# The residual behind layer 0's MLP, added by GpSimd's DMA for two of three token chunks

## The chip, the cores and the metric

The kernel runs on one core of a Trainium2 chip. A core has a matrix engine (TensorE, PE in the profile), a vector engine (VectorE, DVE), a scalar engine (ScalarE, ACT), GpSimd (POOL) and SyncE (SP), each with an instruction queue of its own that is worked off in order, and 16 DMA engines that SP, ACT and POOL can start. The metric is the device time of one execution in microseconds (us).

## What is computed

A two-layer decoder trunk over 1040 tokens (16 learned ones and 1024 of x) and 1024 channels. Each layer is a token mixer and a squared-ReLU MLP, both between RMS norms, and each with a residual. Layer 0 mixes with RWKV-7 and pooling, layer 1 with differential attention. What matters here is the last line of the loop in layer 0 and the first of layer 1:

```python
for i in range(DEPTH):
    hn = rmsnorm(h, g[0])
    m = rwkv_pool_mixer(hn, ...) if i % 2 == 0 else diff_attn_mixer(hn, ...)
    h = h + rmsnorm(m, g[1])
    f = sq_relu_mlp(rmsnorm(h, g[2]), mlp_w1[i], mlp_w2[i])
    h = h + rmsnorm(f, g[3])          # the residual of this document, for i = 0
```

## The kernel before

Tokens lie along the free dimension and channels along the partitions, so that h is eight blocks of 128 channels by 1040 tokens. All matmuls are done in three products of halves (high times high, low times high, high times low), and each operand is therefore cut into a high and a low half.

`late` does the part of a layer from its output projection to the end of its MLP. It does not issue instructions directly: each step is a task of `Flow`, with an engine, a cost, and lists of the pieces that it reads and writes. `Flow.order` then writes down an order for all engines at once: it always takes the task that can start earliest, and of those that can start at the same time the one with the longest way to the end (its rank; a task can be given extra length with `tail`). A DMA counts there with 0.42 us of its queue, then its bytes at 350 GB/s, and 2.0 us more until its data can be used. The order is fixed when the kernel is built; on the chip each engine waits in that order for whatever it needs.

Layer 0's MLP ends in `ac0` and `ac1` (`acc` in the code), 4 blocks of channels each. The end of `late` works in three chunks of tokens (`CH`: 348, 346 and 346, here chunk 0, 1 and 2), and for each of them:

- `down(q)` adds the last product to `ac` (L1053) and sums the squares of the result over the channels (L682 on ACT, L683 on DVE).
- `finish(q)` loads the residual h of the chunk from DRAM into the tiles `hh` with two DMAs of SP (L1062), forms the norm's factor (`rsqrt`, L741 to L743 on ACT, L747 and L748 on DVE), and for each of the eight blocks k multiplies by gain and factor (L1072, DVE) and adds the residual (L1073, DVE). After every second block the two finished blocks are stored to DRAM (L1077), from ACT for chunks 1 and 2.
- `squares(q)` starts the sum of squares for layer 1's first norm: for chunk 0 through the matrix engine, for chunks 1 and 2 block by block into the tile `rsa` (L677 or L682 on ACT, then L683 on DVE).
- `normed(c)` makes layer 1's input: the high halves (L1107, ACT) and the low halves (L1108, DVE). These tasks have a `tail` of 40, 30 and 20 us for chunks 0, 1 and 2, so all that leads to them goes ahead of `squares`, and chunk 1 ahead of chunk 2.

The calls stand in the order `down(0)`, then for each chunk c: `down(c + 1)`, `finish(c)`, `squares(c)`, `normed(c)`. The norm factors of chunk 1 use two small tiles that the squares of `down(2)` use as well, so `finish(1)` begins behind the last square of `down(2)`.

`mixer1` follows, outside `Flow`. Its instructions are ordered by the scheduler of the language; those of `late` keep their order among themselves. Its first matmuls (L377 to L379) project q, k and v of head 0 chunk by chunk. `settle` (L485, with L459 to L463) closes the sum of squares of chunk 1, later of chunk 2, with a matmul over `rsa`. The low half of q's weights (tile `wpx`) is made by the only POOL instruction near this place, L362, which reads two tensors in SBUF.

Of the kernel before, what the change touches and what calls it, by code (L numbers as in the profile page):

```python
# [10 lines left out]
ALU = mybir.AluOpType  # L11
# [3 lines left out]
P = 128  # L15
# [306 lines left out]
class Trunk:  # L322
# [231 lines left out]
    def late(self, l, xs, part, hin, hmid, hout, pre, rsb):  # L554

        nc, tc, A = self.nc, self.tc, self.A
        tt, stt = nc.vector.tensor_tensor, nc.vector.scalar_tensor_tensor
# [13 lines left out]
        def later(make, dt, n):  # L571
            made = {}

            def get(i):
                if i not in made:
                    made[i] = make(i, dt)
                return made[i]

            return [Later(lambda i=i: get(i)) for i in range(n)]

        def use(x):
            return x() if isinstance(x, Later) else x
# [9 lines left out]
        H = [big(i, F32) for i in (0, 1)]  # L592
# [29 lines left out]
        def nC(e, mt, u, v):  # L622
            return [("A", e, mt, a) for a, b in cells if a < v and b > u]

        def nA(e, k):
            return nC(e, k // 2, k % 2 * NH, k % 2 * NH + NH)
# [5 lines left out]
        def nH(i):  # L632
            return [("H", i, k) for k in range(4)]
# [24 lines left out]
        m = AC  # L658
        F = Flow(tc)
# [38 lines left out]
        def free_up(b):  # L698
            held.difference_update(x[1:] for x in b[1])
# [36 lines left out]
        def rsqrt(acc, names, n, y0, t0, ny, nt):  # L736
            vw = sv if len(acc.shape) == 3 else (lambda t: t)

            def a():
                y, t = vw(use(y0)), vw(use(t0))  # L740
                nc.scalar.activation(y, acc, AF.Ln, scale=1.0 / 1024, bias=self.con[:, K_EPS:K_EPS + 1])  # L741
                nc.scalar.activation(y, y, AF.Exp, scale=-0.5)
                nc.scalar.activation(t, y, AF.Square)  # L743

            def v():
                y, t = vw(use(y0)), vw(use(t0))
                stt(t, acc, 1e-6 * 1024, t, op0=ALU.add, op1=ALU.mult)  # L747
                stt(y, t, -3.0 * 1024, y, op0=ALU.add, op1=ALU.mult)  # L748

            F.act(3 * n, a, r=names, w=[ny, nt], k=3)  # L750
            F.dve(2 * n, v, r=names + [ny, nt], w=[ny, nt], k=2)
# [80 lines left out]
        def raw_load(src):  # L832
            r = self.nraw % 2
            self.nraw += 1
            t = R[r]
            F.dma(lambda: nc.sync.dma_start(t.rearrange("p m n -> p (m n)"), src), P * 8192, w=[("R", r, 0), ("R", r, 1)])
            return t, r
# [63 lines left out]
        def weight(i, raw, r, n):  # L901

            a = {(i, e): raw[:, i, 512 * e:512 * e + n] for i in (0, 1) for e in (0, 1)}
            s0, s1 = S[0][:, :n], S[1][:, :n]
            r0, r1 = [("R", r, 0)], [("R", r, 1)]
            if i == 1:
                F.dve(n, lambda: tt(s0, a[1, 0], a[1, 1], op=ALU.add), r=r1, w=[("S", 0)])
                F.dve(n, lambda: tt(s1, s0, a[0, 0], op=ALU.subtract), r=r0 + [("S", 0)], w=[("S", 1)])
                F.dve(n, lambda: tt(a[1, 0], a[0, 0], a[1, 0], op=ALU.subtract), r=r0 + r1, w=r1)
            if i == 3:  # L910
                F.dve(n, lambda: tt(s1, a[0, 1], s1, op=ALU.subtract), r=r0 + [("S", 1)], w=[("S", 1)])
            src, rd = {1: (a[0, 0], r0), 6: (s1, [("S", 1)]), 5: (s0, [("S", 0)]), 2: (a[0, 1], r0),
                       7: (a[1, 0], r1), 3: (s1, [("S", 1)]), 4: (a[1, 1], r1)}[i]
            return one(slot(), src, n, rd)
# [3 lines left out]
        for j in range(14):  # L918
# [4 lines left out]
            raw, r = raw_load(w1[j])  # L923
# [16 lines left out]
            for i in (1, 2, 5, 6, 3, 7, 4) if j == 0 else order:  # L940
                w = weight(i, raw, r, 512)
# [15 lines left out]
            both, nb = flat(ev[:, 1:3]), nA(e, 1) + nA(e, 2)  # L957
# [8 lines left out]
        acc = AC  # L966
# [3 lines left out]
        H3 = later(big, F32, 2)  # L970
# [5 lines left out]
        for b in range(4):  # L976
            nk = 4 if b < 3 else 2
            for q, i in enumerate(order):
                p = place[was[q]]
# [11 lines left out]
            for mp in range(4):  # L991
                raw, r = raw_load(w2[b, mp])
# [10 lines left out]
                for i in order:  # L1003
                    w = weight(i, raw, r, P * nk)
# [6 lines left out]
        for mp in range(4):  # L1011
            r = self.nraw % 2
# [45 lines left out]
        def finish(q):  # L1058
            t0, W = ends[q]
            u, v = t0 - off, t0 - off + W  # L1060
            for x in (0, 1):
                F.dma(lambda x=x: nc.sync.dma_start(use(H3[x][:, :, :W]), self.rows(hmid, t0, W)[:, 4 * x:4 * x + 4]), P * 16 * W, w=nH(x))  # L1062
            a, names = self.sums[q]
            y, t, ny, nt = TT[2][:, :W], T3[1][:, :W], ("T", 2), ("T", 1)
            if q == len(ends) - 1:
                y, t, ny, nt = S[1 - q % 2][:, :W], S[q % 2][:, :W], ("S", 1 - q % 2), ("S", q % 2)
            rsqrt(a, names, W, y, t, ny, nt)
            free_up(self.sums[q])
            rows = self.rows(hout, t0 - off, W)
            for k in range(KT):  # L1070
                d, nd = chunk(k, u, v), nC(k // 4, k % 4, u, v)
                F.dve(W, lambda d=d, k=k: stt(d, d, self.gcol(l, 3, k), y, op0=ALU.mult, op1=ALU.mult), r=nd + [ny], w=nd)  # L1072
                F.dve(W, lambda d=d, k=k: tt(d, d, use(H3[k // 4][:, k % 4, :W]), op=ALU.add), r=nd + [("H", k // 4, k % 4)], w=nd)  # L1073
                if k % 2:
                    src = acc[k // 4].rearrange("p (m h) t -> p m (h t)", h=2)[:, (k - 1) % 4:k % 4 + 1, u:v]
                    other = k % 4 == 3 if l else q > 0
                    F.dma(lambda src=src, k=k, other=other: (nc.scalar if other else nc.sync).dma_start(rows[:, k - 1:k + 1], src), P * 8 * W,  # L1077
                          r=nC((k - 1) // 4, (k - 1) % 4, u, v) + nd, w=[("out", q, k)], eng="ACT" if other else "SP")

        if l:  # L1080
            for q in range(4):
                down(q)
                finish(q)
            F.run()
            stack.close()
            pre.close()
            return None
# [31 lines left out]
        for c in range(3):  # L1119
            if c < 2:  # L1120
                down(c + 1)
            finish(c)
            squares(c)
            normed(c)
# [960 lines left out]
```

## Time and profile before

| What | us |
|---|---|
| median of 3 runs | 2776.96 |
| lowest and highest of them | 2776.26, 2778.88 |
| the profiled execution | 2771.01 |
| its span, from the first to the last instruction | 2769.1 |

All rows below come from the profiled execution and count from the start of its span. A row of the timeline gives start, duration, engine, line of the kernel, operation, the tile written, the tile read, the shape and, in brackets, how long the engine had been idle and who released it. Neighbouring instructions of one kind are merged into one row with a count. "SPq" and "ACTq" are the queues' own DMA instructions.

### The profile page before, as it was taken

What the parts mean: (1) busy time and instruction counts of PE and PEld (TensorE: products, weight loads), DVE (VectorE), ACT (ScalarE), POOL (GpSimd) and SP (SyncE); (2) the same over time, 40 slices, a digit from 0 to 9 for tenths busy, and PEclk for the clock granted to TensorE, in tenths of its full rate; (3) what the DMA queues carried; (4) which work ended last, traced back from release to release, by engine and by line L of the source; (5) the groups of instructions that cost most, each with busy time, mean ns of one, the idle gap of its engine ahead of it and who ended that gap; (6) DMA issues with size and microseconds to landing.
All of it is one profiled execution on the core that took longest, in us unless ns stands there. A gap on an engine that the chain in (4) does not pass through costs nothing.

```text
span 2769.1 us, 44824 instructions
## 1 busy us (share of the span) xinstructions
PE 2614.2 (94%) x16950; PEld 2381.9 (86%) x16950; DVE 2032.5 (73%) x3742; ACT 1342.7 (48%) x2779; POOL 290.4 (10%) x410
## 2 busy tenths in 40 slices
PE   7999998899999999999968999999889999999997
PEld 6899897899899999999956899898787788778877
DVE  5356876534977777888786887888648778778888
ACT  5456776544633334343344556555636333443342
POOL 0111334220000000000012222222000000000000
PEclk9999998899999999999988999999999999999998
DMA  4456777554324345443332222222243243543443
GB/s 152 172 183 187 244 220 222 179 162 150 142 101 170 137 164 193 169 153 132 107 112 73 59 77 68 62 67 62 77 159 137 103 167 150 194 172 137 152 160 122
DMA packets 198575, 391.27 MB, mean 141 GB/s; under 512 B 59984, under 2 KB 122328, under 8 KB 185944
## 3 DMA queue, kind: packets, MB, share of 16 engines
q1 hardware_dynamic: 171176, 348.24, 37.8%
q10 hardware_dynamic: 27184, 40.18, 4.0%
q8 instruction: 133, 2.18, 0.3%
q14 instruction: 82, 0.67, 0.1%
HBM read 240.06 MB, written 131.38 MB: 134 GB/s over the span
## 4 chain that ended last, share of the span: by engine, by line
PE 64%; DVE 10%; ACT 4%; issue 2%; DMA 2%; POOL 0%; DVEq 0%; SPq 0%; ACTq 0%; POOLq 0%
PE bank L691 44%; PE psq L377 2%; PE psq L378 2%; PE psq L379 2%; PE ps L292 1%; PE s L1824 1%; PE tr L1870 1%; PE s L1826 1%; PE xs L292 1%; ACT p L1843 1%; DVE ac L1072 1%; DVE ac L1073 1%; DVE opb L818 1%; PE av L1896 1%; DVE ac L1001 1%
## 5 line engine op out<-in xcount | busy, mean ns | idle before, releaser
L691 PE MATMUL bank<-opa,wp 128*128 128x260 f32 (+1 forms) x3296 | 658.9, 320 | 8.6 <-DVE wp L782 5.3
L691 PEld LDWEIGHTS bank<-opa,wp 128*128 128x128 f32 x3296 | 518.0, 189 | 60.1 <-DVE wp L782 6.8
L691 PE MATMUL bank<-opb,wp 128*128 128x260 f32 (+1 forms) x1150 | 348.4, 324 | 1.8 <-DVE ac L1001 1.8
L292 PE MATMUL ps<-opa,whi 128*128 128x346 f32 (+2 forms) x1008 | 268.3, 328 | 4.7 <-DVE ys L292 4.0
L691 PE MATMUL bank<-opa,hh 128*128 128x260 f32 (+1 forms) x1112 | 241.1, 321 | 8.0 <-DVE hh L782 5.3
L691 PEld LDWEIGHTS bank<-opb,wp 128*128 128x128 f32 x1150 | 216.9, 189 | 21.0 <-ACT opa L1024 2.2
L1001 DVE TENSOR_TENSOR ac<-bank,ac 128x520 f32<-128x520 f32 (+1 forms) x256 | 171.6, 691 | 67.8 <-PE bank L691 66.5
L691 PE MATMUL bank<-opa,opb 128*128 128x260 f32 (+4 forms) x1168 | 206.1, 306 | 11.6 <-ACT opb L670 7.2
L691 PEld LDWEIGHTS bank<-opa,hh 128*128 128x128 f32 x1112 | 185.9, 191 | 24.4 <-DVE hh L782 5.8
L691 PEld LDWEIGHTS bank<-opa,opb 128*128 128x128 f32 x1168 | 168.2, 194 | 22.6 <-ACT opb L670 7.6
L292 PEld LDWEIGHTS ps<-opa,whi 128*128 128x128 f32 x1008 | 181.1, 192 | 6.5 <-DVE ys L292 4.8
L691 PE MATMUL bank<-opb,hh 128*128 128x260 f32 (+1 forms) x616 | 180.6, 327 | 0.0
L781 ACT CAST wp<-raw 128x512 fp32r<-128x512 f32 (+1 forms) x138 | 80.3, 584 | 184.6 <-PE bank L691 179.0
L292 PE MATMUL ps<-opa,wlo 128*128 128x346 f32 (+2 forms) x504 | 158.4, 314 | 0.0
L781 ACT CAST wp<-ss 128x512 fp32r<-128x512 f32 (+1 forms) x130 | 76.7, 590 | 164.5 <-PE bank L691 143.6
L1843 ACT ACTIVATE p<-s,m 128x272 f32<-128x272 f32 (+7 forms) x128 | 95.4, 750 | 85.4 <-DVE m L1839 83.6
L691 PE MATMUL bank<-opa,tt 128*128 128x260 f32 (+1 forms) x648 | 130.5, 318 | 0.2 <-DVE tt L782 0.2
L691 PEld LDWEIGHTS bank<-opb,hh 128*128 128x128 f32 x616 | 117.7, 191 | 9.9
L377 PE MATMUL psq<-opa,wp 128*128 128x346 f32 (+2 forms) x352 | 117.5, 334 | 4.4 <-DVE rp L462 2.6
L362 POOL TENSOR_TENSOR wpx<-raw,wp 128x1024 fp32r<-128x1024 f32 (+1 forms) x14 | 34.4, 2459 | 785.8 <-PE bank L691 742.8
L379 PE MATMUL psq<-opa,wp 128*128 128x346 f32 (+2 forms) x352 | 113.4, 322 | 0.0
L691 PE MATMUL bank<-opb,opb 128*128 128x256 f32 (+4 forms) x456 | 111.3, 308 | 0.5 <-DVE tt L747 0.5
(408 smaller groups left out, 6561.9 us busy)
## 6 DMA issues: line engine op xcount, KB each, us to landing
raw<-in_w_dram SPq DMA_DIRECT2D x64, 1024.0 KB
hid<-ac SPq DMA_DIRECT2D x14, 1820.0 KB
hid<-ac SPq DMA_DIRECT2D x14, 1792.0 KB
hh<-hid SPq DMA_DIRECT2D x23, 1040.0 KB
hh<-hid SPq DMA_DIRECT2D x23, 1024.0 KB
pk<-sg ACTq DMA_DIRECT2D x32, 704.0 KB
lt<-pk SPq DMA_DIRECT2D x32, 704.0 KB
raw<-in_w_qkv_dram SPq DMA_DIRECT2D x24, 512.0 KB
```

What stands on the lines that cost most here:

```text
L292: one = eng, cost, lambda: fn(*args, **kw), r, w
L362: (lo or nc.gpsimd).tensor_tensor(lw[:, :n], raw[:, :n], hi[:, :n].bitcast(F32), op=ALU.subtract)
L377: nc.tensor.matmul(ps, wh, xh, start=(first and i == 0), stop=False)
L378: nc.tensor.matmul(ps, wl, xh, start=False, stop=False)
L379: nc.tensor.matmul(ps, wh, xl, start=False, stop=(last and i == n - 1))
L691: nc.tensor.matmul(ps, use(x), use(y), start=start and i == j == 0, stop=i == len(ws) - 1 and j == 2, skip_group_check=not start)
L781: F.act(n, lambda: nc.scalar.copy(use(t[0][:, :n]), src), r=rd, w=[z[0]] + claim)
L818: F.dve(4 * NH, lambda: tt(lo, use(src), hi.bitcast(F32), op=ALU.subtract), r=rd + wh, w=wl)
L1001: F.dve(NH, lambda d=d, q=q: tt(sv(d), q, sv(d), op=ALU.add), r=nq + nd, w=nd, ps=True)
L1072: F.dve(W, lambda d=d, k=k: stt(d, d, self.gcol(l, 3, k), y, op0=ALU.mult, op1=ALU.mult), r=nd + [ny], w=nd)
L1073: F.dve(W, lambda d=d, k=k: tt(d, d, use(H3[k // 4][:, k % 4, :W]), op=ALU.add), r=nd + [("H", k // 4, k % 4)], w=nd)
L1843: nc.scalar.activation(p[:, :L0], S[c][:, :L0], AF.Exp, bias=m2[:, c:c + 1], scale=0.125, accum_out=m2[:, 2 + c:3 + c])
```

## The change

For chunks 1 and 2 of layer 0, `finish` no longer loads h into `hh` and no longer adds it on DVE. After every second block a DMA started by GpSimd reads two blocks of h from DRAM and adds them to the two blocks in `ac`, in place. The store of the two blocks, `squares` and `normed` then wait for that DMA. Chunk 0, and layer 1, are as before.

```diff
         def finish(q):
             t0, W = ends[q]
             u, v = t0 - off, t0 - off + W
+            plus = not l and q in (1, 2)
             for x in (0, 1):
-                F.dma(lambda x=x: nc.sync.dma_start(use(H3[x][:, :, :W]), self.rows(hmid, t0, W)[:, 4 * x:4 * x + 4]), P * 16 * W, w=nH(x))
+                if not plus:
+                    F.dma(lambda x=x: nc.sync.dma_start(use(H3[x][:, :, :W]), self.rows(hmid, t0, W)[:, 4 * x:4 * x + 4]), P * 16 * W, w=nH(x))
...
                 F.dve(W, lambda d=d, k=k: stt(d, d, self.gcol(l, 3, k), y, op0=ALU.mult, op1=ALU.mult), r=nd + [ny], w=nd)
-                F.dve(W, lambda d=d, k=k: tt(d, d, use(H3[k // 4][:, k % 4, :W]), op=ALU.add), r=nd + [("H", k // 4, k % 4)], w=nd)
+                if plus:
+                    if k % 2:
+                        both = acc[k // 4].rearrange("p (m h) t -> p m (h t)", h=2)[:, (k - 1) % 4:k % 4 + 1, u:v]
+                        nb = nC((k - 1) // 4, (k - 1) % 4, u, v) + nd
+                        F.dma(lambda both=both, k=k: nc.gpsimd.dma_start(both, self.rows(hmid, t0, W)[:, k - 1:k + 1], accum_op=ALU.add), P * 8 * W, r=nb, w=nb, eng="POOL")
+                else:
+                    F.dve(W, lambda d=d, k=k: tt(d, d, use(H3[k // 4][:, k % 4, :W]), op=ALU.add), r=nd + [("H", k // 4, k % 4)], w=nd)
```

## Rows read from the trace of the kernel before

**Rows 1.** The page's first part: busy time, share of the span and number of instructions of each engine.

```profile
span 2769.1 us, 44824 instructions
...
PE 2614.2 (94%) x16950; PEld 2381.9 (86%) x16950; DVE 2032.5 (73%) x3742; ACT 1342.7 (48%) x2779; POOL 290.4 (10%) x410
```

**Rows 2.** Busy time of each engine in four stretches around the change.

```profile
core 0: us, PE busy (x) PEld busy (x) DVE busy (x) ACT busy (x) POOL busy (x), PEclk, DMA share, GB/s
1371.20:1395.70 24.50, 19.56 (x93) 15.16 (x92) 23.09 (x45) 14.60 (x31) 2.65 (x1) 0.94 0.38 116
1395.70:1407.50 11.80, 9.86 (x49) 9.20 (x48) 11.77 (x26) 6.35 (x14) 0.00 (x0) 0.83 0.42 118
1407.50:1423.40 15.90, 0.08 (x1) 0.02 (x1) 15.41 (x34) 7.34 (x16) 0.00 (x0) 0.58 0.89 293
1423.40:1444.80 21.40, 21.34 (x121) 20.59 (x122) 16.77 (x33) 4.98 (x11) 6.50 (x6) 0.92 0.08 26
```

**Rows 3.** The timeline of PE at the end of layer 0.

```profile
1407.24 0.34 PE L379 MATMUL s<-opa,wp 128*128 128x346 f32 x1
1423.41 1.49 PE L485 MATMUL ps<-rsa,con 128*128 128x346 f32 x2 [15.83 <-DVE rsa L683]
1424.19 0.99 PE L378 MATMUL s<-opa,wpx 128*128 128x332 f32 x1
```

**Rows 4.** The timeline of DVE over the same stretch.

```profile
1395.19 0.52 DVE L748 SCALAR_TENSOR_TENSOR tt<-tt,tt 128x346 f32<-128x346 f32 x1
1395.74 4.01 DVE L1072 SCALAR_TENSOR_TENSOR ac<-ac,par,tt 128x346 f32<-128x346 f32 x8
1399.67 3.52 DVE L1073 TENSOR_TENSOR ac<-ac,hh 128x346 f32<-128x346 f32 x8
1403.10 4.01 DVE L1108 SCALAR_TENSOR_TENSOR opa<-ac,par,opa 128x346 fp32r<-128x346 f32 x8
1407.01 0.52 DVE L747 SCALAR_TENSOR_TENSOR ss<-bank,ss 128x346 f32<-128x346 f32 x1
1407.57 0.52 DVE L748 SCALAR_TENSOR_TENSOR ss<-ss,ss 128x346 f32<-128x346 f32 x1
1408.00 0.51 DVE L683 TENSOR_TENSOR rsa<-rsa,tt 128x346 f32<-128x346 f32 x1
1408.43 4.00 DVE L1072 SCALAR_TENSOR_TENSOR ac<-ac,par,ss 128x346 f32<-128x346 f32 x8
1412.35 3.52 DVE L1073 TENSOR_TENSOR ac<-ac,hh 128x346 f32<-128x346 f32 x8
1415.78 4.00 DVE L1108 SCALAR_TENSOR_TENSOR opa<-ac,par,opa 128x346 fp32r<-128x346 f32 x8
1419.70 7.79 DVE L683 TENSOR_TENSOR rsa<-rsa,tt 128x346 f32<-128x346 f32 x13
```

**Rows 5.** The chain that ended last, in order of time (start, us, engine, tile, line), around two places of it.

```profile
1388.32 0.53 DVE ss L683
...
1390.36 2.24 DVE ss L683
1392.63 0.49 ACT tt L682
...
1399.75 3.43 DVE ac L1073 x8
...
1412.43 3.44 DVE ac L1073 x8
...
1422.74 0.53 DVE rsa L683
1423.41 1.49 PE ps L485 x2
```

**Rows 6.** The timeline of POOL from 1380 to 1440 us.

```profile
1389.57 2.65 POOL L362 TENSOR_TENSOR wpx<-raw,wp 128x1024 fp32r<-128x1024 f32 x1 [742.80 <-PE bank L691]
1428.13 2.67 POOL L362 TENSOR_TENSOR spare<-raw,spare 128x1024 fp32r<-128x1024 f32 x1 [35.92 <-ACT spare L361]
...
1434.86 0.90 POOL L1735 TENSOR_TENSOR ab<-ab,rp 128x332 f32<-128x332 f32 x1 [0.70 <-DVE ab L1734]
```

**Rows 7.** The timeline of SP: the loads of `hh` for chunk 2, and the first load of `mixer1`.

```profile
1401.50 2.08 SPq L1062 DMA_DIRECT2D hh<-h  x2
1409.72 0.34 SPq L1650 DMA_DIRECT2D cs<-in_rope_dram  x1
```

**Rows 8.** The first microseconds: a load of 55.5 KB on SP's queue, and DVE's first instruction, which waits for it.

```profile
0.74 0.39 SPq L1973 DMA_DIRECT2D par<-in_par_dram  x1
...
3.86 0.20 DVE L1975 TENSOR_SCALAR par<-par 128x64 f32<-128x64 f32 x1 [3.86 <-DMA par<-in_par_dram]
```

**Rows 9.** The DMA view of three stretches: 1395.7 to 1400, 1401.5 to 1411 and 1407.5 to 1421 us.

```profile
DMA packets 1, 0.02 MB, mean 4 GB/s; under 512 B 0, under 2 KB 0, under 8 KB 0
...
DMA packets 2043, 2.74 MB, mean 288 GB/s; under 512 B 81, under 2 KB 2040, under 8 KB 2040
...
hh<-h SPq DMA_DIRECT2D x2, 692.0 KB
h<-ac ACTq DMA_DIRECT2D x4, 346.0 KB
...
DMA packets 2683, 4.52 MB, mean 335 GB/s; under 512 B 193, under 2 KB 2427, under 8 KB 2555
```

**Rows 10.** The timeline of ACT: the first high half of chunk 2, and one of the stores of chunk 1.

```profile
1403.23 0.45 ACTq L1077 DMA_DIRECT2D h<-ac  x1
...
1412.89 0.58 ACT L1107 ACTIVATE opa<-ac,par 128x346 fp32r<-128x346 f32 x1 [3.85 <-DVE ac L1073]
```

**Rows 11.** Waits of SP's queue from 1300 to 1450 us: who waited for whom, us in total, times, the longest.

```profile
SPq L1650 <- DMA h<-ac: 6.1, 1, 6.1
```

## The prediction, made before the changed kernel was run

> **What bounds the kernel now.** The page's first part comes first: PE is busy 94% of the span, DVE 73% [rows 1]. So DVE work counts only where PE stands still for it. The table by stretches shows one such place [rows 2]: from 1407.5 to 1423.4 PE does 0.08 us of work and DVE 15.41 of 15.90. PE's timeline names the wait [rows 3]: 15.83 us, ended by the last square of chunk 1 going into `rsa` (L683), which `settle` needs. The matmuls of q behind `settle` are ready long before (the low half `wpx` is done at 1392.2 [rows 6]), but PE's order puts `settle` first. DVE's timeline shows what it does meanwhile, without a gap from 1395.74 [rows 4]: scale chunk 1 (8 x L1072), add its residual (8 x L1073), its low halves (8 x L1108), the factor of chunk 2, then the same three for chunk 2, and only then the squares of chunk 1. The chain that ended last runs through all of it [rows 5]. From chunk 1's first scale to `settle` it is 1423.41 - 1395.74 = 27.7 us; that stretch is what the change can shorten.
>
> **What is removed.** The 16 adds: 3.43 and 3.44 us of the chain [rows 5], 6.9 us together, all of it on the path. The loads of `hh` for chunks 1 and 2 go too (2 x 692 KB each [rows 9], SP's row at 1401.5 [rows 7]); DVE didn't wait for them, so that is worth nothing on DVE, but they leave the DMA engines free. Left between chunk 1's first scale and `settle`: 16 scales (8.0), factor of chunk 2 (1.1), 16 low halves (7.8), 7 squares (3.9), 20.8 us.
>
> **What is added: eight POOL DMAs, each between a pair of scales and the high halves.** With its own cost for a DMA (0.42 + 1.0 + 2.0, visible 3.4 us after it can start) the planner orders DVE so, worked out by hand from ranks and tails: 8 scales of chunk 1; factor of chunk 2; its scales 0 and 1; low halves 0 to 5 of chunk 1; scale 2; low halves 6 and 7; scales 3 to 7; low halves 0 and 1 of chunk 2; then squares of chunk 1 mixed with low halves of chunk 2, the last three squares behind them all. Two rounds of DMA thus lie in line: chunk 1's, and pairs 1 to 3 of chunk 2. Let 0 be chunk 1's first scale, L the time from a DMA's start to its data in use, s the spacing of DMAs in a row.
>
> No DMA of POOL is in the trace, so L and s are bounded. L from below: a small load of SP is used 3.86 - 0.74 = 3.1 us after its issue [rows 8]; 346 KB instead of 55.5 at the 335 GB/s that busy DMA engines reach [rows 9] is 0.9 more: 4.0. From above: POOL prepares each DMA as long as its longest instruction here, 2.65 us [rows 6], and the data go through the engines twice, because the old content must be read as well (another 1.1): 7.7. I take 4.6, near the low end: in 1395.7 to 1400 the DMA engines carry 0.02 MB [rows 9], so the first round has them to itself, and 0.6 us is for POOL to prepare the DMA, between SP's issue (0.39 [rows 8]) and POOL's short instruction of 0.90 [rows 6]. For s: one pass at 335 GB/s, 1.06 us, is the low end, a POOL instruction of 2.65 us the high end; I take 1.5, between one pass and two (2.1).
>
> Round 1: pair 0 is scaled at 1.0, leaves at 1.1, is usable at 5.7; the other pairs at 7.2, 8.7, 10.2. A high half (0.58 [rows 10], 0.65 with the handover) stands before each low half. DVE has work until 5.9, so it waits some 0.4 us for pair 0 and about 0.5 for each later one (two low halves take 0.98), less the one scale of 0.5 that fills in, 1.4 us in all: its last low half of chunk 1 ends at 10.2 + 0.65 + 0.98 = 11.8 rather than at 10.4.
>
> Round 2: scale 3 of chunk 2 ends at 12.3, pair 1 leaves at 12.4, is usable at 17.0, pair 3 at 20.0. Stores of chunk 1 and `mixer1`'s load of `cs` share the engines there (335 GB/s before [rows 9]); I add 1.0: 21.0. Behind it stand the last high half and two low ones (1.6) and three squares (1.8): 24.4. In one line, the end is 7.7 + 2L + 5s. DVE's own work would end at 11.8 + 2.5 (scales) + 3.9 (low halves) + 3.9 (squares) = 22.1, or 23.8 to 24.5 with the next point: both ends fall together.
>
> **L362 moves.** It now queues on POOL behind eight DMAs. That it comes later than `late`'s work in program order is seen in PE's order: its reader L378 stands behind `settle` though L362 ran early [rows 3, 6]. Before, it ran at 1389.57 for 2.65 us, and one L683 beside it took 2.24 us instead of 0.53 [rows 5]; the two do not run side by side. So 1.7 us vanish ahead of chunk 1's first scale, and 1.7 to 2.4 come back in round 2, inside DVE's waits there. q's matmuls need it only behind `settle`: hidden if it ends by some 18 to 20; if POOL is later, PE waits for the rest.
>
> By the Trainium skill, page "DMA: Bandwidth & Descriptors", section "Anatomy of one DMA — SWDGE (gpsimd) path", a GpSimd DMA takes about 2.0 us plus bytes at 436 GB/s, an estimated 2.8 us here; L would then be 2.8, round 1 would cost DVE nothing, and the gain would be near (a)'s below. No row shows such a DMA, and SP's 55.5 KB already took 3.1 us [rows 8].
>
> **The sum.** Before 27.7. After 24.4 less the 1.7 at the start is 22.7: 5.0 us gained. Behind `settle` PE is busy 21.34 of 21.40 us [rows 2] and the sums, casts and rotations of DVE, ACT and POOL start from the same event, so all shift by it; PE still begins cold, at 1.2 GHz (clock 0.58 in the hole, half is 0.5 [rows 2]), as before. The profiled execution took 2771.0 (span 2769.1), 5.9 below the median; it would become 2766.0, and the median 2776.96 - 5.0 = 2772.0.
>
> **Rivals.**
> (a) The DMAs are cheap and DVE alone bounds: L 4.0, s 1.06. Round 1 ends at 10.4 without a wait, then 10.3 of DVE's work and 1.7 to 2.4 for L362, less 1.7 at the start: 20.7 to 21.4. Gain 6.3 to 7.0, time 2770.0 to 2770.7. For it: idle DMA engines in round 1. Against it: an add needs the old data too.
> (b) Slower: POOL cannot deliver. Each DMA costs it 2.65 us, by its own length or because DVE's two-input instructions shut POOL out of SBUF, as L362 held up L683 [rows 5, 6]. With L 7.7 and s 2.65 the end is 7.7 + 15.4 + 13.3 = 36.4, less 1.7 is 34.7: 7.0 slower, 2784.0. It is slower than before from 2L + 5s = 21.7 on, as with L 5.5 and s 2.1. For it: eight DMAs in one queue, two rounds in line. Against it: DVE is then waiting and gives room. The Trainium skill, page "SBUF — State Buffer", section "Who interferes with whom", says that GpSimd cannot write DMA descriptors while VectorE runs copies or one-input operations in two-port modes, and that two-input operations shut out only a GpSimd operation that reads SBUF. By that rule (b)'s second reason falls, as L1072, L1108 and L683 have two inputs; the rows of L362, a reader, agree with it, and none shows a writer.
> (c) The gain is given back behind `settle`: `cs`, which SP loads only after chunk 1's first store has landed (6.1 us of wait [rows 11]), or v's low half on POOL (1428.13 [rows 6]) is late next. Against it: that store follows pair 0, usable at 5.7 less 1.7, where it was issued at 1403.23, 7.5 after the first scale [rows 10], beside the loads that go. Gain 0 to 2: 2775 to 2777.
>
> **Chances.** Main case 0.55, its own range 2 to 6.3 us gained (2770.7 to 2775); (a) 0.2; (b) 0.15; (c) 0.1. A difference under 0.2%, 5.6 us, is about what a measurement of this kernel can't tell from none. Faster by more: (a) and 0.14 of the main case, 0.34. Slower by more: 0.12 of (b). Same: 0.54. The range reaches from (a)'s larger gain and half a us for the measurement (the three runs span 2.6) to 2 us slower, the near end of (b): 2769.5 to 2779.
>
> **What would show it.** L1073 with 346 columns is gone; POOL has eight DMA rows; PE's wait before L485 falls from 15.8 to about 11; the L683 near 1390 takes 0.5 us; DVE waits some 1.4 us in round 1 with ACT L1107 as releaser, itself released by a DMA, and little in round 2; L362 follows POOL's last DMA. I am wrong in size if L is far from 4.6 or s from 1.5, and in kind if PE waits after `settle` where it did not.

## The result, and the profile after

The change made the kernel slower by about 6 us: 2782.38 us median against 2776.55 of the kernel before (22 runs each), ratio 1.0023 with a 95% interval of 1.0015 to 1.0032. The forecast was 2772.0 in a range of 2769.5 to 2779. Sign and size are those of rival (b), priced at 2784.0; its mechanism was another.

The lines of the kernel moved by two behind the scale (now L1074) and by eight behind the store: add L1081 (chunk 0 alone), POOL's DMA L1079, high half L1115, low half L1116. PE's timeline at `settle`:

```profile
1430.43 1.49 PE L485 MATMUL ps<-rsa,con 128*128 128x346 f32 x2 [15.91 <-DVE rsa L683]
```

DVE's timeline, from chunk 0's first scale to the last square behind the MLP:

```profile
1376.67 1.07 DVE L1074 SCALAR_TENSOR_TENSOR ac<-ac,par,tt 128x348 f32<-128x348 f32 x2
...
1392.56 1.70 DVE L683 TENSOR_TENSOR ss<-ss,tt 128x346 f32<-128x346 f32 x3
...
1398.29 4.01 DVE L1074 SCALAR_TENSOR_TENSOR ac<-ac,par,tt 128x346 f32<-128x346 f32 x8
...
1406.12 1.07 DVE L1116 SCALAR_TENSOR_TENSOR opa<-ac,par,opa 128x346 fp32r<-128x346 f32 x2 [1.73 <-ACT opa L1115]
1408.81 1.07 DVE L1116 SCALAR_TENSOR_TENSOR opa<-ac,par,opa 128x346 fp32r<-128x346 f32 x2 [1.63 <-ACT opa L1115]
1410.61 1.07 DVE L1116 SCALAR_TENSOR_TENSOR opa<-ac,par,opa 128x346 fp32r<-128x346 f32 x2 [0.72 <-ACT opa L1115]
1411.59 0.57 DVE L1074 SCALAR_TENSOR_TENSOR ac<-ac,par,ss 128x346 f32<-128x346 f32 x1
1412.45 1.07 DVE L1116 SCALAR_TENSOR_TENSOR opa<-ac,par,opa 128x346 fp32r<-128x346 f32 x2 [0.29 <-ACT opa L1115]
1413.44 2.53 DVE L1074 SCALAR_TENSOR_TENSOR ac<-ac,par,ss 128x346 f32<-128x346 f32 x5
1415.89 1.06 DVE L1116 SCALAR_TENSOR_TENSOR opa<-ac,par,opa 128x346 fp32r<-128x346 f32 x2
1416.86 4.48 DVE L683 TENSOR_TENSOR rsa<-rsa,tt 128x346 f32<-128x346 f32 x3
1425.65 1.07 DVE L1116 SCALAR_TENSOR_TENSOR opa<-ac,par,opa 128x346 fp32r<-128x346 f32 x2 [4.30 <-ACT opa L1115]
1426.63 1.14 DVE L683 TENSOR_TENSOR rsa<-rsa,tt 128x346 f32<-128x346 f32 x2
1428.15 1.07 DVE L1116 SCALAR_TENSOR_TENSOR opa<-ac,par,opa 128x346 fp32r<-128x346 f32 x2 [0.38 <-ACT opa L1115]
1429.14 3.47 DVE L683 TENSOR_TENSOR rsa<-rsa,tt 128x346 f32<-128x346 f32 x6
1432.53 1.06 DVE L1116 SCALAR_TENSOR_TENSOR opa<-ac,par,opa 128x346 fp32r<-128x346 f32 x2
1433.50 1.76 DVE L683 TENSOR_TENSOR rsa<-rsa,tt 128x346 f32<-128x346 f32 x3
```

The 16 adds of 346 columns are gone, and the order is nearly the one worked out by hand. But DVE, which had no gap before [rows 4], now waits in both rounds, and PE's hole ends on the same instruction as before [rows 3], no earlier in its own terms: from chunk 1's first scale to `settle` it is 1430.43 - 1398.29 = 32.1 us, against 27.7 before and 24.4 forecast.

POOL's timeline, then ACT's with the high halves, which are the first to use what a DMA has added, and with chunk 1's first store:

```profile
1400.11 6.27 POOL L1079 DMA_DIRECT2D ac<-h  x5 [748.52 <-DVE ac L1074]
1414.31 3.65 POOL L1079 DMA_DIRECT2D ac<-h  x3 [7.93 <-DVE ac L1074]
1417.03 3.31 POOL L362 TENSOR_TENSOR wpx<-raw,wp 128x1024 fp32r<-128x1024 f32 x1
```

```profile
1405.50 1.06 ACT L1115 ACTIVATE opa<-ac,par 128x346 fp32r<-128x346 f32 x2 [6.49 <-DMA ac<-h]
...
1411.83 0.58 ACT L1115 ACTIVATE opa<-ac,par 128x346 fp32r<-128x346 f32 x1 [0.41 <-DMA ac<-h]
1411.91 0.38 ACTq L1085 DMA_DIRECT2D h<-ac  x1
...
1425.03 0.58 ACT L1115 ACTIVATE opa<-ac,par 128x346 fp32r<-128x346 f32 x1 [7.07 <-DMA ac<-h]
```

Round 1: pair 0 is scaled at 1399.3 and used at 1405.5, so L is 6.2; the next three come 2.1 us apart on average, so s is 2.1. Round 2: POOL issues pair 1 at 1414.31, and it is used at 1425.03, 10.7 us later. The DMA view of 1403 to 1412 and of 1414 to 1420.5 us shows why these are different cases (q0 is GpSimd's queue, q10 ACT's stores, q1 SP's loads; packets, MB, and the time that the packets took as a share of 16 engines, which goes over 100% where packets overlap; then an issue row with the median us to landing):

```profile
DMA packets 1212, 1.59 MB, mean 177 GB/s; under 512 B 65, under 2 KB 1211, under 8 KB 1211
...
q0 software_dynamic: 1211, 1.59, 110.3%
...
ac<-h POOLq DMA_DIRECT2D x3, 346.0 KB, 8.6
...
DMA packets 747, 1.80 MB, mean 277 GB/s; under 512 B 33, under 2 KB 630, under 8 KB 630
...
q1 hardware_dynamic: 117, 0.97, 51.8%
q10 hardware_dynamic: 630, 0.83, 40.0%
```

In round 1 the adds have the engines to themselves, keep them full, and move 177 GB/s; other traffic reached 335 before [rows 9]. In the second stretch q0 has no row: none of the adds issued from 1414.31 on has moved, while stores and `cs` take 92% of the engines. That they meet round 2 comes from ACT's order: chunk 1's first store stands behind seven high halves, which wait for the adds, and so it is issued 13.6 us after chunk 1's first scale (7.5 before [rows 10]). Five stores go out from 1411.91 to 1416.13, and SP issues `cs`, which waits for the first of them, at 1414.73.

**The account.** The two profiled executions differ by 10.5 us, 3.9 of it already at chunk 0's first scale (1372.73 before, 1376.67 after), ahead of every edit, so the traces are compared from there. To chunk 1's first scale it is 23.0 us before and 21.6 after: -1.4. To `settle`: +4.5. Behind it, to the last matmul of v's chunk 1 (1455.72 and 1464.67), 32.3 became 34.2: +1.9. Together +5.0, which the interval of the timed difference (4.2 to 8.9 us) holds. The 1.9 us is told of in the last section. Some 1.5 of the 10.5 us are left; they arise later and were not traced.

### The profile page after: what moved, and what is told of

The parts are those of the page before. It is cut to its first block, busy times and chain, and to the rows that moved or that the text cites. A ratio compares the mean times of both kernels' runs of the same rounds, so it can differ in the third digit from the quotient of the medians.

```text
span 2779.7 us, 44839 instructions
## 1 busy us (share of the span) xinstructions
PE 2618.8 (94%) x16950; PEld 2386.2 (86%) x16950; DVE 2031.1 (73%) x3726; ACT 1342.8 (48%) x2779; POOL 301.1 (11%) x418
## 4 chain that ended last, share of the span: by engine, by line
PE 63%; DVE 9%; ACT 4%; DMA 3%; issue 2%; POOL 0%; SPq 0%; DVEq 0%; ACTq 0%; POOLq 0%
PE bank L691 44%; PE psq L377 2%; PE psq L378 2%; PE psq L379 2%; PE ps L292 1%; PE s L1832 1%; PE tr L1878 1%; PE s L1834 1%; PE xs L292 1%; ACT p L1851 1%; DMA ac<-h 1%; PE bank L733 1%; DVE opb L818 1%; PE av L1904 1%; DVE ac L1001 1%
## 5 line engine op out<-in xcount | busy, mean ns | idle before, releaser
L691 PEld LDWEIGHTS bank<-opa,wp 128*128 128x128 f32 x3296 | 517.6, 188 | 59.8 <-DVE wp L782 6.4
L691 PEld LDWEIGHTS bank<-opa,tt 128*128 128x128 f32 x648 | 102.1, 188 | 9.5 <-DVE tt L782 0.4
```

What stands on the lines that cost most here:

```text
L691: nc.tensor.matmul(ps, use(x), use(y), start=start and i == j == 0, stop=i == len(ws) - 1 and j == 2, skip_group_check=not start)
```

## The experiments

All times are read as two distances in each kernel's own trace: A, from chunk 1's first scale to `settle` (L485), and B, from chunk 0's first scale to the end of DVE's last square behind the MLP. The ratio is to the kernel before. The three kernels with copies (plain, plain_one, sp_copy) leave out the MLP's output of chunks 1 and 2; of their intervals only plain's ends below 1.

| kernel | A, us | B, us | ratio (95%) |
|---|---|---|---|
| before | 27.7 | 54.8 | 1 |
| the change | 32.1 | 58.6 | 1.0023 (1.0015 to 1.0032) |
| plain | 24.9 | 51.3 | 0.9983 (0.9967 to 0.9999) |
| plain_one | 23.4 | 50.2 | 0.9985 (0.9969 to 1.0001) |
| sp_copy | 20.7 | 48.9 | 0.9987 (0.9971 to 1.0002) |
| late_store | 32.3 | 60.9 | 1.0027 (1.0012 to 1.0041) |
| late_both | 27.9 | 56.4 | 1.0030 (1.0018 to 1.0042) |
| wpx_dve | 33.3 | 59.8 | 1.0035 (1.0018 to 1.0052) |
| c1_only | 29.7 | 55.4 | 1.0004 (0.9995 to 1.0013) |
| c2_only | 28.6 | 54.9 | 1.0004 (0.9990 to 1.0017) |
| sq_before | 17.9 | 53.8 | 0.9997 (0.9986 to 1.0008) |
| sq_after | 20.7 | 59.9 | 1.0023 (1.0010 to 1.0037) |
| sq_pool | 17.9 | 53.8 | 1.0003 (0.9990 to 1.0017) |
| sq_pool_c2 | 17.9 | 53.6 | 1.0002 (0.9987 to 1.0016) |

The theory was that the adds are slow on the DMA engines (theory E); the rival that POOL is slow (theory P).

### The DMAs without the add: plain, plain_one, sp_copy

Shown is the issuing call alone, without the task around it (in sp_copy the task's engine becomes SP as well).

```diff
-nc.gpsimd.dma_start(both, self.rows(hmid, t0, W)[:, k - 1:k + 1], accum_op=ALU.add)
+nc.gpsimd.dma_start(both, self.rows(hmid, t0, W)[:, k - 1:k + 1])    # plain
+nc.gpsimd.dma_start(dj, self.rows(hmid, t0, W)[:, j])                # plain_one: j = k - 1, then k
+nc.sync.dma_start(both, self.rows(hmid, t0, W)[:, k - 1:k + 1])      # sp_copy
```

> The changed kernel, with its eight GpSimd DMAs copying the two blocks of h over those of ac instead of adding to them (so the MLP's output of chunks 1 and 2 is left out, and all else runs as in the changed kernel). Measure: from chunk 1's first scale to settle's matmul, 27.7 us before, 32.1 in the changed kernel. Theory E (the DMA engines): an add of 346 KB keeps the engines busy for 1.75 us because it does twice the work of a copy; copies then come 1.0 us apart in round 1 rather than 1.8, and the DMA view shows the software queue at over 300 GB/s rather than 200; round 1 ends 2.4 us earlier and the measure falls to 28 to 30. Theory P (POOL's own preparation): the spacing is POOL's 1.2 us or more per DMA and stays at 1.8, and the measure stays within 1 us of 32.1.

> As the run with GpSimd's copies (MLP output of chunks 1 and 2 left out), but the eight copies are started by SP. Theory E: round 1's spacing is that of GpSimd's copies; only the way from the issue to the first data is shorter, by 1 us or less, and the measure is within 3 us of the run with GpSimd's copies. Theory P: each round loses POOL's preparation, 2 to 3 us in round 1 and, as L362 is no longer behind the DMAs, 4 or more in round 2: the measure is 25 or less. The load of cs stands behind the copies in SP's queue here, so round 2 is free of it, which E would count as up to 3 us (1040 KB at 335 GB/s).

> GpSimd's copies without the add again (MLP output of chunks 1 and 2 left out), but one block per DMA, sixteen of them, not eight of two blocks. In the run with copies of two blocks the packets were 3.3 KB and the first round moved at 321 GB/s; with the adds they are 1.3 KB at 177 GB/s, and SP's copies had 1.3 KB as well. So the copy differed from the add in its packets too. If adding is what halves the rate, packets of 1.3 KB without the add cost the engines about what SP's did (0.07 us each, against 0.13 with the add), and round 1 moves at over 250 GB/s unless POOL's sixteen instructions are then the bound. If it was the packet size on GpSimd's queue, they cost 0.12 us or more each, and round 1 stays at about 180 to 200 GB/s.

Round 1 of plain in the DMA view (1402 to 1407 us), of sp_copy (1399 to 1405), of plain_one (1397 to 1402):

```profile
DMA packets 492, 1.60 MB, mean 321 GB/s; under 512 B 64, under 2 KB 128, under 8 KB 491
...
q0 software_dynamic: 491, 1.60, 93.6%
...
ac<-h POOLq DMA_DIRECT2D x3, 346.0 KB, 3.9
```

```profile
q1 hardware_dynamic: 1146, 1.50, 85.6%
```

```profile
q0 software_dynamic: 493, 1.34, 87.1%
```

The copy lands 3.9 us after its issue, where the add takes 8.6 in the changed kernel's view of its round 1 (medians of three in a row; the quickest of round 1 landed after 3.7 and 5.3); it moves 321 GB/s, not 177. In plain DVE waits for round 1 only twice, 0.17 and 0.26 us. L is 4.65 (scaled at 1399.0, used at 1403.62), and round 1 ends 11.1 us after chunk 1's first scale, where 4.6 and 11.8 were forecast: what the prediction described there is GpSimd's copy, not its add. A falls to 24.9, half a us from the forecast of 24.4, but that is partly chance: pair 1 of chunk 2 is usable after 19.9 us, not 18.0, and 4.9 us follow it, not 6.4. Theory E holds and P falls for round 1; E's 28 to 30 was still too high. POOL's own time falls with the add as well, from one DMA every 1.25 us to 0.72 to 0.80 each. It did not space the adds, though: they came 2.1 us apart, with the DMA engines full. sp_copy shows what was priced as rival (a): A is 20.7, the bound by DVE's work that was put at 20.7 to 21.4. Its first copy is used 3.1 us after SP issues it (1398.09 to 1401.15), plain's 3.8 after POOL's issue (1399.81 to 1403.62). In round 2 the two differ by much more (0.74 us of wait against 4.38): A is 4.2 below plain's, outside the 3 that E allowed and inside P's "25 or less". In sp_copy `cs` is issued behind the copies (1414.81), in plain just ahead of round 2 (1409.60); whether that makes the difference or the queue does was not separated.

One thing stays open. On average the adds travel in packets of 1.3 KB (1.59 MB / 1211), plain's in 3.3 KB; plain_one was to bring them to 1.3 and has 2.7, so it did not make its test. SP's copies have 1.3 KB and cost the engines 6.0 x 16 x 0.856 / 1146 = 0.072 us each, the adds 9.0 x 16 x 1.103 / 1211 = 0.131. So GpSimd's adding DMA costs the engines nearly twice as much per packet as SP's copy. Worked out per KB it is 0.100 us for the adds, 0.055 for SP's copies, and 0.047 (plain) and 0.052 (plain_one) for GpSimd's: neither GpSimd's queue alone nor the packet size alone doubles the price. A copy in packets of 1.3 KB on GpSimd's queue was not run, so the share of the add itself is not shown.

### What held up round 2: wpx_dve, late_store, late_both

```diff
-w[nme] = self.weights(self.A["w_qkv"][8 if nme == "k" else 0])
+w[nme] = self.weights(self.A["w_qkv"][8 if nme == "k" else 0], lo=nc.vector)    # wpx_dve
```
```diff
+                    if not l and q == 1:
+                        kept.append(store)
+                    else:
+                        store()
...
+        for s in kept:
+            s(nhx(KT * 2 + 7, 1))
...
+            nc.vector.tensor_copy(self.cs[:, 0, 0:1], self.rsa[:, T - 1:T])
```

Here `store` is the DMA task of L1085 with a list of further pieces that it is planned to read (chunk 2's last low half). The last line, ahead of the load of `cs`, is in late_both alone.

> The changed kernel, with the low half of q's weights (L362, wpx) made by DVE behind late's work, not by POOL behind the DMAs. Theory E: the measure stays within 1 us of 32.1, as L362 was only waiting beside the transfers. Theory P: what held back round 2 was L362 in POOL's queue or on POOL's port; without it the data start some 3 us earlier, ACT's wait for pair 1 falls from 7.1 to about 4, and the measure to 28.5 to 29.5. Behind settle PE waits for wpx, which DVE makes only then (1.1 us or more), in both.

> The changed kernel, with the four stores of chunk 1 planned behind the last low half of chunk 2, so that they and the load of cs, which waits for the first of them, no longer share the DMA engines with round 2. Theory E: the second round's first data come some 2.2 us after POOL's first issue, as in round 1, not 6; ACT's wait for pair 1 falls from 7.1 to 3 to 4 us, and the measure from 32.1 to 28 to 29. Theory P: round 2's data still begin only when L362 is done, ACT's wait stays at 6 to 7, and the measure at 31 to 33. The whole kernel gains less than the measure, since cs comes later behind settle.

> The run with chunk 1's stores planned late, and in addition the load of cs made to wait for DVE's last square behind the MLP (a one-column copy into cs in front of it), so that round 2 has the DMA engines to itself. With the stores late but cs not, pair 1 was usable 5.0 us after POOL's issue and then cs took the engines at 1416.7, so that pair 2 came 6.3 us behind pair 1. Theory E (round 2 is late because stores and cs stand ahead of it and beside it on the DMA engines): pairs 1, 2 and 3 are usable 5 to 5.5 us after POOL's issue and then 1.8 to 2.2 us apart, as in round 1, and the measure from chunk 1's first scale to settle falls from 32.1 to 26 to 28: still no less than about the 27.7 of before, because round 1 is the same. Rival (the second round is slow for a reason of its own on POOL or in the queue): the measure stays above 30. Behind settle cs is late in both, so the whole kernel gains nothing or loses.

In the trace of the change round 2's first packets move when L362 ends (1420.34), which is also when `cs` thins out, so both theories could claim it. wpx_dve takes L362 away from POOL, and ACT waits longer for pair 1, not shorter (A is 33.3, 0.2 more than E allowed):

```profile
1423.86 0.59 ACT L1115 ACTIVATE opa<-ac,par 128x346 fp32r<-128x346 f32 x1 [7.91 <-DMA ac<-h]
```

POOL issues there at 1412.30, and in the DMA view from there to 1420 its queue moves 0.10 MB, beside 2.00 MB of stores and loads.

late_both takes the stores and `cs` away instead. POOL's timeline of its round 2, then ACT's (POOL's DMA is L1081 here, the high half L1121):

```profile
1409.91 3.65 POOL L1081 DMA_DIRECT2D ac<-h  x3 [8.22 <-DVE ac L1076]
1412.62 3.32 POOL L362 TENSOR_TENSOR wpx<-raw,wp 128x1024 fp32r<-128x1024 f32 x1
```

```profile
1415.21 1.06 ACT L1121 ACTIVATE opa<-ac,par 128x346 fp32r<-128x346 f32 x2 [1.65 <-DMA ac<-h]
1417.79 1.06 ACT L1121 ACTIVATE opa<-ac,par 128x346 fp32r<-128x346 f32 x2 [0.31 <-DMA ac<-h]
1419.60 0.59 ACT L1121 ACTIVATE opa<-ac,par 128x346 fp32r<-128x346 f32 x1 [0.37 <-DMA ac<-h]
```

Pair 1 is used 5.3 us after its issue, while L362 is still running, and the others 2.6 and 1.8 us later. A is 27.9, inside the 26 to 28 expected by E. Theory P falls: POOL issued in time, and its adds got no share of the engines until most of the stores and of `cs` had moved. late_store alone was half a step: pair 1 came 5.0 us after its issue (1414.77 to 1419.73), but then `cs` took the engines and pair 2 came only at 1426.01; A stayed at 32.3, not E's 28 to 29. Neither makes the kernel faster. In both, DVE's last squares wait for ACT (2.48 us in late_both, 2.58 in late_store), whose order has the postponed stores ahead of them, and in late_both DVE then waits another 2.24 us for `cs`.

### One chunk alone: c1_only, c2_only

```diff
-plus = not l and q in (1, 2)
+plus = not l and q == 1      # c1_only
+plus = not l and q == 2      # c2_only
```

> The change for chunk 1 alone; chunk 2 is added by DVE. Theory E: round 1 is as in the changed kernel (ends 15 us after chunk 1's first scale, of which 4 to 5 are waits), then come DVE's own 2.5 (scales), 3.4 (adds), 3.9 (low halves) and 3.6 (squares): the measure is 28 to 29, and with the 1.4 us that L362 no longer costs ahead of it the kernel stays within 0.1% of before. Rival (the loss of the changed kernel is in round 1): 1.002 or more of the time before.

> The change for chunk 2 alone; chunk 1 is added by DVE. DVE then has no wait before its scales of chunk 2 end, 16.5 us after chunk 1's first scale, and five of chunk 1's seven squares fall into the wait, but the last two stand behind low halves of chunk 2's pairs 1 to 3. Theory E: chunk 1's stores and cs are on the DMA engines when POOL's four DMAs are issued, so the data come 8 us or more behind the issue and the measure is 27 to 30: same as before or up to 3 us slower. Rival (round 2 was late only because round 1 pushed it there): the data come after 5 to 6 us and the measure is 23 to 25, 3 to 5 us faster than before.

Each alone makes no difference that can be measured. c1_only is 0.7 us over E's 28 to 29: L362 fell on DVE's scales, and two of them took 5.12 us (1397.13) where two took 1.07 in the change. In c2_only A is inside E's 27 to 30, but not for E's reason: POOL issued the first DMA at 1413.11 and its data were used at 1418.07, after 5.0 us and not 8, because chunk 1's stores, issued from 1406.09 to 1408.45, no longer stood ahead of it: from 1413.5 us on ACT's queue has no row in the DMA view. The time went to L362 beside DVE's squares, three of which took 5.72 us (1415.20). So the sharing is no property of chunk 2: it comes when the second round's DMAs are issued together with the first round's stores, as the change does with both chunks.

### Is settle the bound? sq_before, sq_after, sq_pool, sq_pool_c2

```diff
-rank[i] = span[i] + max([rank[j] for j in succ[i]], default=T[i][6])
+rank[i] = span[i] + max([T[i][6]] + [rank[j] for j in succ[i]])
...
-                square(chunk(k, t0, t0 + W), out, W, nC(k // 4, k % 4, t0, t0 + W), k == 0, [("sum", q)])
+                square(chunk(k, t0, t0 + W), out, W, nC(k // 4, k % 4, t0, t0 + W), k == 0, [("sum", q)], tail=26.0 if q == 1 else 0.0)
...
-w["v"] = self.weights(self.A["w_qkv"][16 + h], pool=spare)
+w["v"] = self.weights(self.A["w_qkv"][16 + h], pool=spare, cast=None if h else nc.gpsimd.tensor_copy)
```

The first two edits are in all four kernels, the last in sq_pool and sq_pool_c2.

> The kernel before, without the change, but with chunk 1's squares planned in front of chunk 2's adds (a tail of 26 us on them, and a rank that counts a tail also for a task with successors). My reading of the hole is that PE waits for chunk 1's squares only because they stand last in DVE's order, not because DVE has too much to do. If so, settle starts about 18 to 19 us after chunk 1's first scale instead of 27.7, PE then has q of chunks 0 and 1 to do while DVE does chunk 2, and the kernel gains 4 to 8 us (0.998 to 0.997). If DVE's whole work bounds instead, PE waits as long for chunk 2's low halves, and the time is within 0.1% of before.

> The changed kernel with chunk 1's squares planned early, as was done to the kernel before in sq_before. Settle then no longer waits for the second round of DMAs: it starts 20 to 21 us after chunk 1's first scale (32.1 in the changed kernel, 17.9 in sq_before). If settle's wait were the whole loss, the kernel would gain some 5 us over the changed one. What I learned from sq_before speaks against that: v's weights are cast by ACT behind all of late's squares, and chunk 2's squares still wait for round 2, so v starts no earlier than 37 us after chunk 1's first scale, and the first matmul of k's or q's chunk 2 (50.2 us in the changed kernel, 45.2 before) comes at 48 to 50: 0 to 2 us better than the changed kernel, 1.0015 to 1.0025 of before.

> sq_before with one more edit: the high half of v's weights of head 0 (spare) is cast by POOL, which is idle there, and not by ACT behind late's squares. In sq_before PE stood still for 3.7 us for that cast and 1.9 us for the low half behind it. If this is where sq_before's gain went, both waits go, the first matmul of chunk 2 comes 37 to 40 us after chunk 1's first scale (44.0 in sq_before, 45.2 before), and the kernel takes 0.9975 to 0.9985 of before. If DVE's ropes or the load of v's weights are late next, the ratio stays within 0.001 of 1.

> As sq_pool, with the change for chunk 2 alone: the residual of chunk 2 added by GpSimd's DMAs. Here PE has q and v of chunks 0 and 1 to do while the DMAs run, some 20 us from settle on, so their latency should be hidden, and DVE does 3.4 us less. Theory E: chunk 2's low halves come 1 to 3 us later than in sq_pool for the contention with stores and cs, PE does not feel it, and the time is that of sq_pool within 0.1%. Rival (POOL's queue): the cast of v's weights now stands behind four DMAs and L362 on POOL, PE waits for it, and the kernel is 2 to 5 us slower than sq_pool.

`settle` moved as expected in all four (A 17.9 to 20.7), and the gains forecast for sq_before (4 to 8 us) and sq_pool did not come; sq_after is as slow as the change, and sq_pool_c2 takes sq_pool's time. PE's timeline of sq_before shows where the gain went:

```profile
1417.00 1.49 PE L485 MATMUL ps<-rsa,con 128*128 128x346 f32 x2 [6.10 <-DVE rsa L683]
...
1430.25 0.62 PE L377 MATMUL psv<-opa,spare 128*128 128x348 f32 x1 [3.67 <-ACT spare L361]
1432.75 0.66 PE L378 MATMUL psv<-opa,spare 128*128 128x348 f32 x1 [1.88 <-POOL spare L362]
```

PE does q and then stands still for v's weights, whose cast ACT does only behind the last squares. Casting them early on POOL (sq_pool) moved the wait to the low half: PE waited 5.99 us for POOL's L362, and that began at 1428.32, just as DVE's last square ended. In sq_pool_c2 the row names that releaser outright:

```profile
1426.41 2.72 POOL L362 TENSOR_TENSOR spare<-raw,spare 128x1024 fp32r<-128x1024 f32 x1 [7.74 <-DVE rsa L683]
```

So my reading of the hole was only half right. L683 ends PE's wait, but behind it a second wait is tied to the last square of chunk 2, and the times follow B, the whole of DVE's list, rather than A. In the table B is 48.9 to 51.3 for the three kernels with ratios of 0.9983 to 0.9987, 53.6 to 55.4 for the even ones, and 58.6 or more for the change, late_store, wpx_dve and sq_after; late_both, with `cs` late, is the exception. That B bounds is read from this table; no run moved B alone, and why the low half of v's weights waits for that square was not tested. No version that does all the work is shown to beat the kernel before.

## Why the prediction was wrong, step by step

- **Right:** the place (a hole ended by L683), the adds that go, the two rounds in line. Chunk 1's last squares stand behind pair 2's low halves, not behind pair 3's as I had it; the hand-made order was wrong there, in the forecast's disfavour.
- **Right in kind, a little off in size:** L362 moved behind POOL's DMAs. The L683 that it had held up took 2.24 us [rows 5], now three take 1.70, and chunk 1's first scale came 1.4 us earlier relative to chunk 0's (1.7 forecast). It came back in round 2 (1417.03, beside three L683 of 4.48 us), where DVE waits anyway, as forecast.
- **The step that failed, first part: the price of an add.** I took L 4.6 and s 1.5, near the low ends, because the engines are free in round 1. They were free, and the add still took L 6.2 and s 2.1. Round 1 ended 15.2 us after chunk 1's first scale (the last low half, 1412.45 + 1.07), not 11.8: +3.4, of which 1.6 is L and 3 x 0.6 is s. DVE waited 4.4 us there (1.73, 1.63, 0.72 and 0.29), not 1.4. The copies of plain show that the numbers suited a copy. The bounds of 4.0 to 7.7 and 1.06 to 2.65 held the truth; I chose the wrong end, with an argument about traffic and none about the add.
- **Second part: sharing in round 2.** I added 1.0 us for stores and `cs`. Pair 1 took 10.7 us from issue to use, 5.3 with the engines free: the sharing cost 5.4 there and 32.1 - 27.9 = 4.3 at `settle`. Together, pair 1 was usable 26.7 us after chunk 1's first scale and not 18.0 (17.0 and the 1.0): 3.4 of the 8.7 are round 1, 5.3 are round 2. From there to `settle` it was 5.4 us and not 6.4, as the last squares stood behind pair 2: 32.1.
- **Third part: "all shift by it".** Behind `settle` another 1.9 us was lost, 1.3 of it to the granted clock of this one execution (last section).
- **Rival (b)** named the sign, the size and the point, 2L + 5s over 21.7; with L of 6.2 and 10.7 and s of 2.1 the sum is 6.2 + 10.7 + 10.5 = 27.4. (With the 7.7 that makes 35.1; less the 1.0 for sharing, which is in the 10.7, and one s, as the squares did not wait for pair 3, it is 32.0, and 32.1 was measured.) Its mechanism is not what happened: POOL got through a DMA every 6.27 / 5 = 1.25 us in round 1, not 2.65, and was done in time. So that 2784.0 lies near the measured 2782.4 is partly luck. By the Trainium skill, page "SBUF — State Buffer", section "Who interferes with whom", DVE's two-input instructions don't keep GpSimd from writing descriptors, which the page calls inferred. The traces agree as far as they go: beside L1074 and L683 single DMA instructions of POOL took 1.19 and 1.20 us in sq_after, and none reached 2.65 in the changed kernel.
- **Rival (a)** happened to the hardware copies of sp_copy, with A of 20.7. **Rival (c)** did not: nothing on PE waited for `cs`. The reason given against it was wrong all the same: chunk 1's first store came 13.6 us after its first scale, not earlier than the 7.5 of before.

The Trainium skill's figure for a GpSimd DMA, page "DMA: Bandwidth & Descriptors", section "Anatomy of one DMA — SWDGE (gpsimd) path", came to an estimated 2.8 us. Measured from issue to landing it is 3.9 for the copy and 8.6 for the add in round 1 (medians of three in a row); the measurement decides.

## What to carry to other kernels

Price a DMA that adds by a run of its own or at the far bound: here it took the engines nearly twice as long as a copy, and its data came 6 us behind the last scale even with the engines free. Ask of every transfer put on a chain what its predecessors will send out at the same moment: the second round's adds moved only when most of the first round's stores had. And before a wait is shortened, look for the next one tied to the same end; PE's hole was named by one square, yet moving that square 10 us forward gained nothing.

## What the runs showed of the hardware

The granted clock took part. Rows by stretch: before, the 7.58 us from the first matmul behind PE's 2.60 us wait to the last matmul of v's chunk 1; after, the same work.

```profile
1448.14:1455.72 7.58, 7.58 (x47) 7.58 (x48) 4.76 (x9) 1.05 (x1) 3.41 (x3) 1.00 0.44 127
```

```profile
1455.78:1464.67 8.89, 8.89 (x47) 8.89 (x48) 4.74 (x9) 1.05 (x1) 3.39 (x3) 0.84 0.51 137
```

The same 47 matmuls took 1.3 us more, at a granted clock of 0.84 rather than 1.00: part of them ran at 1.2 GHz and not at 2.4. The other 0.6 of the 1.9 us lies between `settle` and the first matmul of chunk 2: 17.48 us at a clock of 0.90 before, 18.09 at 0.88 after, 0.31 of it a wait for v. sq_before shows the slower form too (9.10 us at 0.81). Why the clock fell behind the same wait of 2.60 us in one kernel and not in the other stays open.
